# Two-layer decoder trunk on one core: input projection of the unnormalized h, with the norm's factor applied to its banks

## The chip, the cores and the metric

The kernel runs on one core of a Trainium2 chip. The metric is the device time of one execution in microseconds. A core has TensorE (PE in the profile; its weight loads are PEld), VectorE (DVE), ScalarE (ACT), GpSimd (POOL) and SyncE (SP), which here issues every DMA. Each engine has its own queue and works it off in order; an instruction that waits for another engine holds up all that stand behind it. SBUF is the on-chip memory that all of them use; PSUM is where PE's products are summed, in banks of 128 x 512 fp32 numbers.

## The reference

```python
D_MODEL = 1024; SEQ = 1024; DEPTH = 2; NORM_EPS = 1e-6

def rmsnorm(x, g):
    y = x * lax.rsqrt(jnp.mean(x * x, axis=-1, keepdims=True) + NORM_EPS)
    return y * g

for l in range(DEPTH):
    u = rmsnorm(h, attn_norm[l])
    rq, rk, rv, rg, dq, dk, dv = jnp.split(u @ w_in[l], offsets, axis=-1)
    ret  = retention(rq, rk, rv), normed per head, times silu(rg)   # 4 heads
    diff = differential_attention(dq, dk, dv), normed per head      # 4 heads, causal, ALiBi
    h = h + concat(ret, diff) @ w_out[l]
    h = h + swiglu(rmsnorm(h, ffn_norm[l]))
out = rmsnorm(h, final_norm)
```

The line that matters is `u = rmsnorm(h, attn_norm[l])` with the projection behind it. A token's norm factor y = rsqrt(mean(h²) + eps) is one number per token, the gain g one number per channel, so u = h · g · y, and u @ w_in = y · ((h · g) @ w_in), row by row.

## The kernel before, in words

**Layout.** h is kept transposed: eight tiles of 128 channels by 1024 tokens (names a_1 to a_8 and the like in the trace). The tokens are worked in two halves of 512. Products are fp32-accurate ones made of three passes: each operand is split into a rounded high part and the rest (low), and `mm3` issues high x high, high x low and low x high (L268 to L270; L303 to L305 for values, with tokens as rows and 256 columns each). A bank of the projection is thus 8 channel tiles x 3 = 24 products of 512 columns, or 48 of 256 columns. There are three banks called `ps_mm` in rotation for them.

**Weights** come by DMA as raw tiles (`wr`) and are split by `weight`: ACT rounds the high half (L260), POOL subtracts it for the low half (L261).

**The norm** of a half is `norm_half` with two helpers. `squares`: ACT squares each of the eight tiles (L406, into tiles `kb`), DVE adds them up in `acc` (L413). `rsqrt_rows`: PE sums over channels (L378, four matmuls with a column of ones), DVE and ACT make the factor of each token as a column (nx, ny, L383 to L390), PE spreads it by four transposes into a row that is the same on all partitions (L394, in PSUM, `ps_s`). Then `norm_half` makes u: DVE multiplies h · g · y (L426, with y read from PSUM), ACT rounds the high part (L428), DVE subtracts for the low part (L430). The number that its generator yields (lag, gap) is how much other PE work is issued before the row sums and before the transposes.

**What the projection's banks go to.** `stack` takes the q or k bank of a differential head: ACT copies its two halves of 64 rows with a scale (L502) and DVE makes the low parts (L503), all at high priority in the scheduler. `values` copies a bank (ACT, L526) and subtracts (DVE, L527). In the retention `ret_proj` copies the q and k banks (ACT), the values are copied (ACT, L735) and the gates go through ACT's silu (L336).

**Order.** PE's order is written out by hand: generators issue products and yield the number they issued, and `weave(main, n, fill, m)` interleaves two of them in proportion. In `attention` the projection of a head's q and k runs as fill between the parts of the head before. The order on ACT, DVE, POOL and SP is set by a scheduler that follows the program order and priorities.

**The start** of layer 0 is special. `run` loads the weights of the first k and q stacks and half 0 of x in turns; DVE multiplies the gain into these weights (L1195), and `fm_first` (L287) multiplies them with the plain h of half 0, in unsplit fp32, while the norm is being made. When the norm is there, its row is multiplied into the two banks (L672). `keep` gives two of half 0's low parts to POOL. The values of half 0, woven with the norm of half 1, follow, and then head 0, woven with the stacks of half 1.

**From layer to layer**, half 0 of the next layer's norm runs within the last products of the layer before; half 1 is woven with the first stacks of the new layer.

Of the kernel before, what the change touches and what calls it, by code (L numbers as in the profile page):

```python
# [144 lines left out]
class Trunk:  # L145
# [136 lines left out]
    def fm_first(self, h, ws):  # L282

        for w in ws:
            ps = self.bank("mm")
            for k in range(KT):
                self.nc.tensor.matmul(ps, lhsT=w[:, P * k:P * k + P], rhs=h[k][:, 0:HT], start=k == 0,  # L287
                                      stop=k == KT - 1)
                yield 4
            self.first_ps.append(ps)  # L290

# [79 lines left out]
    def rsqrt_rows(self, parts, dim, cols=HT, gap=14):  # L371
# [18 lines left out]
        nc.vector.scalar_tensor_tensor(out=y, in0=x, scalar=1.5, in1=y, op0=ALU.add, op1=ALU.mult)  # L390
        yield gap
# [24 lines left out]
    def norm_half(self, h, hf, gcol, us, lag=11, gap=9, first=False, keep=False):  # L416
        nc = self.nc
        sl = slice(hf * HT, hf * HT + HT)
        parts = self.squares(h, sl, 0, True, first)
        yield lag  # L420
        y = yield from self.rsqrt_rows(parts, D, gap=gap)
        hi = self.t("u", 4, [P, KT, HT], R32)
        lo = self.t("u", 4, [P, KT, HT], R32)
        for k in range(KT):
            f = self.tmp()
            nc.vector.scalar_tensor_tensor(out=f, in0=h[k][:, sl], scalar=self.gains[:, gcol + k:gcol + k + 1],  # L426
                                           in1=y, op0=ALU.mult, op1=ALU.mult)
            nc.scalar.copy(hi[:, k], f)  # L428
            eng = nc.gpsimd if keep and k in (1, 4) else nc.vector
            eng.tensor_tensor(out=lo[:, k], in0=f, in1=hi[:, k].bitcast(F32), op=ALU.subtract)  # L430
        if keep:
            self.first_y = self.big("sp")[:, 0:HT]
            nc.scalar.copy(self.first_y, y)
        us[hf] = (hi, lo)
# [70 lines left out]

    def stacks(self, w, us, halves, st, scale):
        for hf in halves:
            ps = yield from self.fm_half(w, us[hf])
            self.stack(ps, st, slice(hf * HT, hf * HT + HT), scale)
# [8 lines left out]
    def values(self, w2, us, hf, v, pairs=(0, 1)):  # L518
# [4 lines left out]
        for t2 in pairs:  # L523
            ps = yield from self.tm_pair(w2, us[hf], 2 * t2)
            sl = slice(512 * t2, 512 * t2 + 512)
            nc.scalar.copy(h[:, sl], ps)  # L526
            nc.vector.tensor_tensor(out=o[:, sl], in0=ps, in1=h[:, sl].bitcast(F32), op=ALU.subtract)  # L527
# [135 lines left out]
    def attention(self, l, us, w_first, norm1):  # L663
# [5 lines left out]
        if l == 0:  # L669
            for ps, st, scale in zip(self.first_ps, (qk[1], qk[0]), (1.0, 0.125)):  # L670
                f = self.tmp()
                nc.vector.tensor_tensor(out=f, in0=ps, in1=self.first_y, op=ALU.mult)  # L672
                self.stack(f, st, slice(0, HT), scale)
            self.weave(norm1, 40, self.values(wdv, us, 0, v), 48)
# [4 lines left out]
        for h in range(4):  # L679
# [7 lines left out]
            if h == 0:  # L687
                self.weave(self.att_part(l, A, 0, 4), PART0, first[1], 96)
# [23 lines left out]
    def ret_proj(self, us, dst, scale):  # L712
        w = self.weight()
        for hf in range(NH):
            ps = yield from self.fm_half(w, us[hf])
            self.nc.scalar.activation(dst[:, hf * HT:hf * HT + HT], ps, AF.Copy, scale=scale)

    def retention_inputs(self, us, rq, rk, close):
# [8 lines left out]
        for p in range(2):  # L727
            w2, todo = [self.weight(), self.weight()], []
            for hf in range(NH):
                for t2 in range(2):  # L730
                    dst = rv[2 * hf + t2].rearrange("p (t f) -> p t f", t=2)[:, :, 256 * p:256 * p + 256]

                    def go(dst=dst, hf=hf, t2=t2):
                        ps = yield from self.tm_pair(w2, us[hf], 2 * t2)
                        nc.scalar.copy(dst, ps.rearrange("p (t f) -> p t f", t=2))  # L735
# [6 lines left out]
        for h in range(4):  # L742
            w = self.weight()
            for hf in range(NH):
                def go(hf=hf, h=h):
                    ps = yield from self.fm_half(w, us[hf])
                    for c in range(2):
# [430 lines left out]
    def run(self):  # L1178
# [4 lines left out]
        fold = [self.big("sp") for _ in range(2)]  # L1183
# [6 lines left out]
        def load_w(i, c):  # L1190
            cs = slice(512 * c, 512 * c + 512)
            nc.sync.dma_start(raws[i][:, cs], self.a["wts"][i][:, cs])
# [11 lines left out]
        for c in range(2):  # L1204
            load_w(1, c)
# [47 lines left out]
```

## Time and profile before

| | us |
|---|---|
| median of 3 runs | 2317.77 (2315.94 to 2318.31) |
| the profiled execution | 2316.4 |
| its span in the trace | 2314.6 |
| PE busy | 2265.0 (98%) |
| DVE busy | 1389.3 (60%) |
| ACT busy | 1010.4 (44%) |
| POOL busy | 781.0 (34%) |

1.8 us of the profiled execution lie outside the span. In a row of the timeline stand the start, the duration, engine and line, the operation, what it writes and reads, its shape, how often it came in a row, and in brackets the idle time of that engine before it and what ended it. The busy time of a PE instruction (0.39 us for a 512-column product) is longer than the step from one to the next, since they are pipelined; the step is read from the start times. In a table by stretches the columns are the length, then for PE, PEld, DVE, ACT and POOL the busy time and the number of instructions, then the granted clock of PE (1.00 is full), the DMA share and GB/s.

### The profile page before, as it was taken

Reading aid. Unit: us, or ns where it says so; the run is one execution under the profiler, and the core shown is the slowest. Engines: PE = TensorE matmul, PEld = TensorE weight load, DVE = VectorE, ACT = ScalarE, POOL = GpSimd, SP = SyncE. Lnnn points to the kernel's source line nnn. Section 1 sums busy time; section 2 is a strip of 40 time slices with the busy share of each in tenths; the row PEclk is TensorE's granted clock in tenths of the full one; section 3 lists DMA queues with packets and bytes.
Section 4 is the critical chain, followed back from the end, with each engine's and each line's share of the span. In section 5 each row is a group of like instructions: output and inputs, shape, how many; then the busy total and the mean of one; then the engine's idle time right before and its main releaser. Section 6 shows DMA issues by size and latency. Waiting matters only on the chain.

```text
span 2314.6 us, 30688 instructions
## 1 busy us (share of the span) xinstructions
PE 2265.0 (98%) x11328; PEld 1900.0 (82%) x11328; DVE 1389.3 (60%) x2564; ACT 1010.4 (44%) x1905; POOL 781.0 (34%) x620
## 2 busy tenths in 40 slices
PE   8999999998999999999999999999999999999998
PEld 5888898887888888888888888988778888888887
DVE  8777612987534333895567775059874343349856
ACT  5666523444333333543346665234443333344332
POOL 3111212123445455335221112211245445544350
PEclk9999999999999999999999999999999999999999
DMA  4212121111332332652222122212123232346522
GB/s 164 76 47 65 44 94 37 55 56 55 130 116 93 112 105 92 227 195 88 81 84 55 48 72 74 64 37 73 48 91 121 78 128 78 107 162 187 168 64 73
DMA packets 74215, 216.58 MB, mean 94 GB/s; under 512 B 8017, under 2 KB 10065, under 8 KB 74065
## 3 DMA queue, kind: packets, MB, share of 16 engines
q1 hardware_dynamic: 74064, 214.62, 28.7%
q8 instruction: 89, 1.46, 0.3%
q14 instruction: 62, 0.50, 0.1%
HBM read 162.16 MB, written 44.04 MB: 89 GB/s over the span
## 4 chain that ended last, share of the span: by engine, by line
PE 82%; DVE 12%; ACT 3%; issue 2%; DMA 1%; POOL 0%; SPq 0%; DVEq 0%; ACTq 0%; POOLq 0%
PE ps_mm L244 8%; PE ps_mm L246 8%; PE ps_mm L245 8%; PE ps_mm L268 7%; PE ps_mm L269 7%; PE ps_mm L270 7%; PE ps_s L244 5%; PE ps_s L246 5%; PE ps_s L245 5%; PE ps_mm L305 2%; PE ps_mm L303 2%; PE ps_mm L304 2%; PE ps_t L246 2%; PE ps_t L245 2%; PE ps_t L244 2%
## 5 line engine op out<-in xcount | busy, mean ns | idle before, releaser
L221 POOL TENSOR_TENSOR w<-wr,w 128x512 fp32r<-128x512 f32 x286 | 401.9, 1417 | 532.1 <-ACT w L220 492.1
L261 POOL TENSOR_TENSOR w<-wr,w 128x512 fp32r<-128x512 f32 x140 | 184.7, 1326 | 576.9 <-ACT w L260 550.5
L268 PE MATMUL ps_mm<-u,w 128*128 128x512 f32 (+1 forms) x735 | 296.6, 404 | 0.0
L269 PE MATMUL ps_mm<-u,w 128*128 128x512 f32 (+1 forms) x735 | 287.7, 391 | 0.9 <-DVE u L430 0.9
L270 PE MATMUL ps_mm<-u,w 128*128 128x512 f32 (+1 forms) x735 | 287.8, 392 | 0.0
L220 ACT CAST w<-wr 128x512 fp32r<-128x512 f32 x312 | 188.1, 619 | 134.5 <-DVE wr L887 72.0
L245 PE MATMUL ps_mm<-u,w 128*128 128x512 f32 x432 | 168.3, 390 | 0.0
L246 PE MATMUL ps_mm<-u,w 128*128 128x512 f32 x432 | 168.2, 389 | 0.0
L244 PE MATMUL ps_mm<-u,w 128*128 128x512 f32 x432 | 168.2, 389 | 0.0
L270 PEld LDWEIGHTS ps_mm<-u,w 128*128 128x128 f32 x735 | 138.4, 188 | 30.5
L269 PEld LDWEIGHTS ps_mm<-u,w 128*128 128x128 f32 x735 | 138.8, 189 | 24.4 <-DVE u L430 1.2
L268 PEld LDWEIGHTS ps_mm<-u,w 128*128 128x128 f32 x735 | 138.7, 189 | 24.2
L935 ACT COPY t<-ps_mm 128x512 f32<-128x512 f32 x76 | 44.6, 587 | 254.0 <-PE ps_mm L246 254.0
L260 ACT CAST w<-wr 128x512 fp32r<-128x512 f32 x140 | 85.9, 619 | 133.9 <-PE ps_mm L269 42.8
L303 PE MATMUL ps_mm<-w,u 128*128 128x256 f32 x448 | 128.8, 288 | 0.0
L304 PE MATMUL ps_mm<-w,u 128*128 128x256 f32 x448 | 127.7, 285 | 0.0
L305 PE MATMUL ps_mm<-w,u 128*128 128x256 f32 x448 | 127.6, 285 | 0.0
L557 DVE CUSTOM_DVE_ANT_0 sp<-ps_s,wr 128x512 f32<-128x512 f32 (+2 forms) x192 | 103.1, 551 | 35.1 <-PE ps_s L555 34.0
L561 ACT ACTIVATE sp<-sp,m 128x256 f32<-128x256 f32 (+7 forms) x128 | 99.1, 775 | 52.0 <-DVE m L560 51.3
L845 DVE TENSOR_TENSOR a<-a,ps_mm 128x512 f32<-128x512 f32 (+1 forms) x148 | 98.6, 666 | 33.5 <-PE ps_mm L246 20.1
L885 DVE TENSOR_TENSOR t<-wr,wr 128x512 f32<-128x512 f32 x46 | 35.2, 766 | 119.7 <-DMA wr<-wts 119.7
L244 PE MATMUL ps_s<-u,w 128*128 128x512 f32 x264 | 102.9, 390 | 3.4 <-ACT t L935 3.4
(379 smaller groups left out, 5930.9 us busy)
## 6 DMA issues: line engine op xcount, KB each, us to landing
wr<-wts SPq DMA_DIRECT2D x190, 512.0 KB, 3.7
mx<-s_fast SPq DMA_DIRECT2D x56, 512.0 KB, 4.8
s_fast<-mx SPq DMA_DIRECT2D x48, 512.0 KB, 5.0
kb<-ka SPq DMA_DIRECT2D x64, 128.0 KB, 2.3
s_rest<-mx SPq DMA_DIRECT2D x12, 512.0 KB, 2.9
kb<-wts SPq DMA_DIRECT2D x12, 512.0 KB, 5.9
mx<-s_rest SPq DMA_DIRECT2D x12, 512.0 KB, 3.7
a<-xT SPq DMA_DIRECT2D x16, 256.0 KB, 5.4
```

The source lines that it names most:

```text
L220: nc.scalar.copy(h, src)
L221: (eng or nc.gpsimd).tensor_tensor(out=o, in0=src, in1=h.bitcast(F32), op=ALU.subtract)
L244: mm(ps, lhsT=wh[:, c], rhs=bh, start=first and i == 0, stop=False, skip_group_check=True)
L245: mm(ps, lhsT=wh[:, c], rhs=bl, start=False, stop=False, skip_group_check=True)
L246: mm(ps, lhsT=wl[:, c], rhs=bh, start=False, stop=i == 3, skip_group_check=True)
L261: nc.gpsimd.tensor_tensor(out=o, in0=raw[:, cols], in1=h.bitcast(F32), op=ALU.subtract)
L268: mm(out, lhsT=lh, rhs=rh, start=first, stop=False)
L269: mm(out, lhsT=lh, rhs=rl, start=False, stop=False)
L270: mm(out, lhsT=ll, rhs=rh, start=False, stop=last)
L303: mm(o, lhsT=uh, rhs=wh, start=k == 0, stop=False)
L304: mm(o, lhsT=uh, rhs=wl, start=False, stop=False)
L305: mm(o, lhsT=ul, rhs=wh, start=False, stop=k == KT - 1)
```

## The change

- u no longer holds the norm's factor. `norm_half` first makes the high part of h · g on ACT (L416 of the change) and the low part on DVE (L417), for both of which nothing of the norm is needed, and only then squares and sums. The factor is kept twice: as a row (copied from PSUM into an `acc` tile, ACT L423) and as the columns ny.
- Where a bank is read, the factor goes in: the stacks' and gates' banks are multiplied by the row into a `t2` tile first (`normed`, DVE L500, at high priority); `ret_proj` does it in one DVE operation in place of the ACT copy; values and retention values, whose rows are tokens, take a column as the scale (two operations of 256 columns, ACT L525 and DVE L526, in place of one of 512).
- The folded weights and `fm_first` are gone. The first k and q stacks of half 0 are split products like all others, with `weight` called first, and the norm of half 0 is issued between them and the values. POOL has no part in u any more.
- `run` issues the DMAs in another order: all of the first two weights with half 0 of x, then the two values weights, then half 1 of x.

```diff
@@ fm_first (removed)
-        for w in ws:
-            ps = self.bank("mm")
-            for k in range(KT):
-                self.nc.tensor.matmul(ps, lhsT=w[:, P * k:P * k + P], rhs=h[k][:, 0:HT], start=k == 0,
-                                      stop=k == KT - 1)
-                yield 4
-            self.first_ps.append(ps)
@@ rsqrt_rows
+        self.cols = y
         yield gap
@@ norm_half
-    def norm_half(self, h, hf, gcol, us, lag=11, gap=9, first=False, keep=False):
+    def norm_half(self, h, hf, gcol, us, lag=11, gap=9, first=False):
+        hi = self.t("u", 4, [P, KT, HT], R32)
+        lo = self.t("u", 4, [P, KT, HT], R32)
+        us[hf] = [hi, lo, None, None]
+        for k in range(KT):
+            g = self.gains[:, gcol + k:gcol + k + 1]
+            nc.scalar.mul(hi[:, k], h[k][:, sl], g)
+            nc.vector.scalar_tensor_tensor(out=lo[:, k], in0=h[k][:, sl], scalar=g, in1=hi[:, k].bitcast(F32),
+                                           op0=ALU.mult, op1=ALU.subtract)
         parts = self.squares(h, sl, 0, True, first)
         yield lag
         y = yield from self.rsqrt_rows(parts, D, gap=gap)
-        for k in range(KT):
-            f = self.tmp()
-            nc.vector.scalar_tensor_tensor(out=f, in0=h[k][:, sl], scalar=self.gains[:, gcol + k:gcol + k + 1],
-                                           in1=y, op0=ALU.mult, op1=ALU.mult)
-            nc.scalar.copy(hi[:, k], f)
-            eng = nc.gpsimd if keep and k in (1, 4) else nc.vector
-            eng.tensor_tensor(out=lo[:, k], in0=f, in1=hi[:, k].bitcast(F32), op=ALU.subtract)
...
+        row = self.t("acc", 2, [P, 512])
+        nc.scalar.copy(row, y)
+        us[hf][2:] = [row, self.cols]
@@ stacks
+    def normed(self, ps, u):
+        f = self.tmp()
+        with self.tc.high_priority():
+            self.nc.vector.tensor_tensor(out=f, in0=ps, in1=u[2], op=ALU.mult)
+        return f
+
     def stacks(self, w, us, halves, st, scale):
         for hf in halves:
             ps = yield from self.fm_half(w, us[hf])
-            self.stack(ps, st, slice(hf * HT, hf * HT + HT), scale)
+            self.stack(self.normed(ps, us[hf]), st, slice(hf * HT, hf * HT + HT), scale)
@@ values
-            nc.scalar.copy(h[:, sl], ps)
-            nc.vector.tensor_tensor(out=o[:, sl], in0=ps, in1=h[:, sl].bitcast(F32), op=ALU.subtract)
+            for b in range(2):
+                sl, src = slice(512 * t2 + 256 * b, 512 * t2 + 256 * b + 256), ps[:, 256 * b:256 * b + 256]
+                y = us[hf][3][:, 2 * t2 + b:2 * t2 + b + 1]
+                nc.scalar.mul(h[:, sl], src, y)
+                nc.vector.scalar_tensor_tensor(out=o[:, sl], in0=src, scalar=y, in1=h[:, sl].bitcast(F32),
+                                               op0=ALU.mult, op1=ALU.subtract)
@@ attention, layer 0
-            self.weave(norm1, 40, self.values(wdv, us, 0, v), 48)
+            (lag, norm0), norm1 = norm1
+            def main():
+                yield lag
+                yield from norm0
+                for ps, st, scale in zip(got, (qk[1], qk[0]), (1.0, 0.125)):
+                    self.stack(self.normed(ps, us[0]), st, slice(0, HT), scale)
+            self.weave(main(), 96, self.chain(one(wk), one(wq), self.values(wdv, us, 0, v)), 96)
+            next(norm1)
...
-                self.weave(self.att_part(l, A, 0, 4), PART0, first[1], 96)
+                self.weave(self.chain(norm1, self.att_part(l, A, 0, 4)), PART0, first[1], 96)
@@ ret_proj
-            self.nc.scalar.activation(dst[:, hf * HT:hf * HT + HT], ps, AF.Copy, scale=scale)
+            self.nc.vector.scalar_tensor_tensor(out=dst[:, hf * HT:hf * HT + HT], in0=ps, scalar=scale, in1=us[hf][2],
+                                                op0=ALU.mult, op1=ALU.mult)
@@ retention gates
                     ps = yield from self.fm_half(w, us[hf])
+                    ps = self.normed(ps, us[hf])
```

PE at the start. Before, rows from the middle of the second unsplit bank to the first values products (`ps_mm_180` is that bank, `ps_mm_295` a values bank, `acc_155` the squares of half 1):

```order
17 L287 MATMUL ps_mm_180<-a_7_82,sp_87 128x512
18 L287 MATMUL ps_mm_180<-a_8_83,sp_87 128x512
19 L378 MATMUL ps_s_281<-c_ones,acc_155 128x1 x4
20 L303 MATMUL ps_mm_295<-w_248,u_188 128x256
21 L304 MATMUL ps_mm_295<-w_249,u_188 128x256
```

and of the change, from the last products of the q stack to the transposes (`ps_mm_249` is the first values bank, `acc_123` the squares of half 0):

```order
46 L268 MATMUL ps_mm_209<-u_105,w_150 128x512
47 L269 MATMUL ps_mm_209<-u_106,w_150 128x512
48 L270 MATMUL ps_mm_209<-u_105,w_151 128x512
49 L368 MATMUL ps_s_235<-c_ones,acc_123 128x1 x4
50 L293 MATMUL ps_mm_249<-w_156,u_105 128x256
...
73 L295 MATMUL ps_mm_249<-mx_166,u_106 128x256
74 L385 MATMUL ps_s_274<-c_ident,ny_241 128x128 x4
75 L293 MATMUL ps_mm_249<-w_156,u_105 128x256
```

Before, the row sums of half 1 stand ahead of the values; now those of half 0 do, with the transposes 24 products behind, and the sums of half 1 come after the values.

ACT at the end of the values of half 0, in the change (`ps_mm_321` is the second values bank, `kb_412` the last square of half 1):

```order
47 L397 ACTIVATE kb_403<-a_5_80 128x512
48 L397 ACTIVATE kb_406<-a_6_81 128x512
49 L397 ACTIVATE kb_409<-a_7_82 128x512
50 L525 ACTIVATE v_247<-ps_mm_321,ny_241 128x256
51 L199 ACTIVATE c_ex<-c_dots 128x4
52 L397 ACTIVATE kb_412<-a_8_83 128x512
53 L525 ACTIVATE v_247<-ps_mm_321,ny_241 128x256
```

The last square of half 1 stands behind the first copy out of the second values bank.

DVE at the passage from layer 0 to layer 1. Before, around the last add to h (`a_691_3901` is the last tile of h, `acc_9990` the squares of half 1, `u_9818` the low part of half 0):

```order
1243 L426 SCALAR_TENSOR_TENSOR t_1761_9847<-a_691_3901,c_gains,ps_s_9812 128x512
1244 L430 TENSOR_TENSOR u_9818<-t_1760_9843,u_9817 128x512
1245 L413 TENSOR_TENSOR acc_9990<-acc_9990,kb_10007 128x512
1246 L845 TENSOR_TENSOR a_691_3901<-a_691_3901,ps_mm_9925 128x512
1247 L430 TENSOR_TENSOR u_9818<-t_1761_9847,u_9817 128x512
1248 L413 TENSOR_TENSOR acc_9990<-acc_9990,kb_10010 128x512
1249 L383 TENSOR_SCALAR nx_10026<-ps_s_10027 128x4
```

and in the change (`a_696_3964` is that tile, `acc_10057` the squares, `u_10040` the low part of half 1):

```order
1256 L404 TENSOR_TENSOR acc_10057<-acc_10057,kb_10074 128x512
1257 L858 TENSOR_TENSOR a_696_3964<-a_696_3964,ps_mm_9974 128x512
1258 L417 SCALAR_TENSOR_TENSOR u_10040<-a_689_3957,c_gains,u_10039 128x512
1259 L417 SCALAR_TENSOR_TENSOR u_10040<-a_690_3958,c_gains,u_10039 128x512
1260 L404 TENSOR_TENSOR acc_10057<-acc_10057,kb_10077 128x512
1261 L417 SCALAR_TENSOR_TENSOR u_10040<-a_691_3959,c_gains,u_10039 128x512
...
1266 L417 SCALAR_TENSOR_TENSOR u_10040<-a_696_3964,c_gains,u_10039 128x512
1267 L373 TENSOR_SCALAR nx_10093<-ps_s_10094 128x4
```

The operations on half 0 are gone from between the adds; two L417 of half 1 stand ahead of the last add, and six behind it, ahead of the reading of the row sums.

57 lines of the change are left out of this document (17 added, 40 removed).

## The prediction

> **What bounds the kernel now.** I read the page's busy shares first, then what PE waited for over the whole span, then the two stretches in which the long waits lie.
>
> ```profile
> PE 2265.0 (98%) x11328; PEld 1900.0 (82%) x11328; DVE 1389.3 (60%) x2564; ACT 1010.4 (44%) x1905; POOL 781.0 (34%) x620
> ...
> PE ps_s L378 <- DVE acc L413: 8.2, 4, 4.1
> PE ps_mm L287 <- DMA a<-xT: 5.3, 1, 5.3
> PE ps_o L269 <- DVE a L586: 3.3, 8, 0.7
> PE ps_t L580 <- DVE sp L642: 2.5, 2, 1.3
> PE ps_s L554 <- DVE m L557: 1.1, 2, 0.5
> PE ps_mm L269 <- DVE u L430: 0.9, 1, 0.9
> ```
>
> The first line is busy time: PE works 2265.0 of 2314.6 us, so at most 49.6 us of idle time can be won, and beyond that only PE's own work and its clock. In the waits the columns are the sum, the number of waits and the longest. The first is the one that this change is about: PE stands in front of the row sums of squares (L378) because the last add of squares is late, 8.2 us in four places. The two long ones are at the start and at the passage from layer 0 to layer 1:
>
> ```profile
> 5.27 8.24 PE L287 MATMUL ps_mm<-a,sp 128*128 128x512 f32 x12 [5.27 <-DMA a<-xT]
> ...
> 27.82 1.79 PE L378 MATMUL ps_s<-c_ones,acc 128*128 128x1 f32 x8 [2.95 <-DVE acc L413]
> ...
> 31.96 0.41 PE L305 MATMUL ps_mm<-w,u 128*128 128x256 f32 x1
> 32.18 0.41 PE L303 MATMUL ps_mm<-mx,u 128*128 128x256 f32 x1
> ...
> 46.15 0.28 PE L305 MATMUL ps_mm<-mx,u 128*128 128x256 f32 x1
> 46.27 0.40 PE L268 MATMUL ps_mm<-u,w 128*128 128x512 f32 x1
> 46.50 0.40 PE L269 MATMUL ps_mm<-u,w 128*128 128x512 f32 x1
> ```
> ```profile
> 20.00:30.00 10.00, 7.05 (x22) 4.10 (x21) 9.90 (x14) 7.30 (x13) 6.15 (x4) 0.89 0.26 91
> 30.00:40.00 10.00, 9.10 (x48) 8.64 (x47) 9.03 (x18) 4.63 (x9) 3.44 (x3) 0.59 0.54 149
> 40.00:50.00 10.00, 10.00 (x71) 9.35 (x70) 9.91 (x17) 6.31 (x12) 1.02 (x5) 1.00 0.13 34
> ```
>
> The second fence is the table by stretches (length, then busy time of PE, weight loads, DVE, ACT and POOL, then the granted clock). After the wait of 2.95 us the clock was 0.59 for the next 10 us: a 256-column product starts every 0.22 us there (31.96, 32.18) and every 0.12 at 46.15. That is 10 x 0.41 = 4.1 us lost beside the wait itself. DVE is busy for over 9 of 10 us in all three stretches. The first stack of half 1 starts at 46.27, and 0.9 us more is lost in it (the L269 wait above): **47.2 us** is the mark that the changed start has to beat. The step between 512-column products is 0.23 us (46.27, 46.50).
>
> The passage between the layers, PE, then the stretch as a whole, and DVE:
>
> ```profile
> 1159.11 0.40 PE L268 MATMUL ps_mm<-u,w 128*128 128x512 f32 x1
> ...
> 1161.62 0.39 PE L270 MATMUL ps_mm<-u,w 128*128 128x512 f32 x1
> 1166.06 1.83 PE L378 MATMUL ps_s<-c_ones,acc 128*128 128x1 f32 x8 [4.06 <-DVE acc L413]
> ...
> 1169.18 0.63 PE L268 MATMUL ps_mm<-u,w 128*128 128x512 f32 x1
> 1169.61 0.63 PE L269 MATMUL ps_mm<-u,w 128*128 128x512 f32 x1
> ...
> 1171.57 0.60 PE L394 MATMUL ps_s<-c_ident,ny 128*128 128x128 f32 x4
> ```
> ```profile
> 1160.00:1170.00 10.00, 5.94 (x22) 4.84 (x21) 6.57 (x13) 3.40 (x7) 2.75 (x2) 0.73 0.73 247
> ```
> ```profile
> 1158.56 1.77 DVE L413 TENSOR_TENSOR acc<-acc,kb 128x512 f32<-128x512 f32 x1
> ...
> 1163.38 0.68 DVE L845 TENSOR_TENSOR a<-a,ps_mm 128x512 f32<-128x512 f32 x1
> 1163.97 1.34 DVE L430 TENSOR_TENSOR u<-t,u 128x512 fp32r<-128x512 f32 x1
> 1165.23 0.68 DVE L413 TENSOR_TENSOR acc<-acc,kb 128x512 f32<-128x512 f32 x1
> 1167.93 0.16 DVE L383 TENSOR_SCALAR nx<-ps_s 128x4 f32<-128x4 f32 x1 [2.02 <-PE ps_s L378]
> ...
> 1169.00 0.16 DVE L390 SCALAR_TENSOR_TENSOR ny<-nx,ny 128x4 f32<-128x4 f32 x1
> ```
>
> The output products of layer 0 end where the first product of layer 1 starts, 1159.11. Up to the transposes (1171.57) PE needs 12.46 us for 21 products and the row sums. DVE is behind by some 4 us: its adds and the halves' own multiplications and subtractions (L426, L430) stand in one queue, and with two operands in SBUF some took 1.34 to 1.77 us in place of 0.68.
>
> **The change part by part.** The prices, from the groups of the first 60 us (count, sum, mean ns):
>
> ```profile
> L287 PE MATMUL ps_mm<-a,sp 128*128 128x512 f32 x32 | 17.2, 695 | 5.3 <-DMA a<-xT 5.3
> L261 POOL TENSOR_TENSOR w<-wr,w 128x512 fp32r<-128x512 f32 x9 | 13.1, 1462 | 15.4 <-ACT w L260 15.4
> L426 DVE SCALAR_TENSOR_TENSOR t<-a,c_gains,ps_s 128x512 f32<-128x512 f32 x16 | 11.3, 739 | 0.8 <-PE ps_s L394 0.8
> L406 ACT ACTIVATE kb<-a 128x512 f32<-128x512 f32 x14 | 8.7, 628 | 3.3 <-DVE acc L413 1.9 <-DMA a<-xT 1.2
> L260 ACT CAST w<-wr 128x512 fp32r<-128x512 f32 x10 | 6.0, 614 | 6.3 <-PE ps_mm L269 2.4 <-DMA wr<-wts 2.2 <-issue 1.6
> L526 ACT CAST v<-ps_mm 128x512 fp32r<-128x512 f32 x2 | 1.2, 580 | 0.0
> L527 DVE TENSOR_TENSOR v<-ps_mm,v 128x512 fp32r<-128x512 f32 x2 | 1.4, 680 | 0.0
> L672 DVE TENSOR_TENSOR t<-ps_mm,sp 128x512 f32<-128x512 f32 x2 | 1.3, 678 | 0.0
> ```
>
> *Start.* Removed: the unsplit products, 17.2 us of PE, and DVE's folding of the weights. Added: 48 split products, 48 x 0.23 = 11.0 us. So PE has 6.2 us less to do, but it now needs operands that ACT, DVE and POOL make. I lay the new order out in time. PE starts when the first tile is there (5.27) and is split (one ACT operation, 0.63): 5.9. ACT's next twelve operations, casts, squares and splits, take 12 x 0.63 = 7.6, which gives 12.9; the last low part on DVE (priced as L426, 0.74) and late tiles make it 14 to 15, so wk's bank ends at about 15.5. ACT casts the second half of wq as its seventeenth operation, 5.27 + 17 x 0.63 = 16.0; POOL needs 1.46 for it, with a queue ahead, so it is there at 17.5 to 18.2, and the last twelve products of wq end at 21 to 22. The row sums take 1 us, to 22 to 23. The first half of a values bank, 24 x 0.12 = 2.9, ends at 25 to 26. Now the transposes (L385 of the change) wait: between the sums and ny DVE does four L417 of half 1 and four short operations. At 0.74 that is 4 x 0.74 + 0.6 = 3.6 us; at 1.34 (the L430 row at 1163.97, since L417 reads two tiles of SBUF beside POOL's splits) it is 6.0. So ny is ready at 26 to 28.5: **a new wait of 0.5 to 3 us**. Transposes 0.6, the second half 2.9, the second bank 5.7: values end at 35.5 to 38. There the next wait stands: half 1's last square is queued on ACT behind the first copy out of that bank (L525), so after PE's last product come copy (at most 0.58), square 0.63, add 0.68 and the hand-overs, about **2.4 us**. With sums and transposes of half 1 (1.6, which before lay ahead of the mark) the mark is reached at 39.5 to 42 at full clock: 5 to 7.5 us gained. If the wait for L385 is as long as the one of 2.95, the clock can fall as it did there, 4.1 us. Bounds of the gain: 1 and 7.5. I take **4.5**: nearer the upper end, because the longer of the new waits is under 2.95 in the middle of its range.
>
> On that clock the Trainium skill ("TensorE: Matmul & The Clock Gate", What's actually happening) says that the gate closes after about 3.4 us without work, in windows that run freely. By that rule both new waits leave the clock alone and the gain would be 5 to 7.5; the trace agrees only in part, since the 2.95 us above lowered it.
>
> *Passage between the layers.* DVE no longer has L426 and L430 between the adds. After the last product of the output (call it t) come the add to h 0.68, two L417 that are queued ahead (2 x 0.68), the last add 0.68: the sums can start at t + 3.0, where PE's 12 products end at t + 2.8 (12 x 0.23). Nearly all of the 4.06 goes. But six L417 stand ahead of nx on DVE: t + 3.0 + 6 x 0.68 = t + 7.1, then 1.2 us for the chain from nx to ny (1167.93 to 1169.16), t + 8.3, while PE's 9 products end at t + 6.1. So **a new wait of about 2.2** at the transposes, which stand at t + 8.4 to 9.2 in place of t + 12.46. Gain 3.3 to 4.1; with the six L417 at 1.34 it falls by 4 to about 0. I take **3.0**, most of the cover being DVE alone (POOL has 2 operations in 1160 to 1170).
>
> *Banks.* Per layer DVE gets 16 multiplications for the q and k stacks, 8 for the gates and 8 for the retention's q and k (these replace an ACT copy), each 0.68 as L672: 22 us; each values bank becomes two operations of half the size on ACT and two on DVE, which adds about the 0.16 that a tiny operation takes (L390's row). What covers them is PE's own time: 24 products, 5.5 us, to a bank, and three banks. It covers them where DVE has room, and in attention it has little:
>
> ```profile
> 80.00:100.00 20.00, 20.00 (x106) 16.98 (x105) 16.98 (x46) 14.26 (x28) 2.80 (x3) 1.00 0.09 27
> 120.00:140.00 20.00, 18.35 (x98) 14.94 (x97) 18.62 (x60) 14.98 (x33) 2.63 (x2) 1.00 0.10 28
> ```
>
> At 17.0 of 20 us PE has no idle time; at 18.6 it has 1.65. PE's attention waits on DVE (L586, L642, L557 in the first fence) are 6.9 us in 12 waits for both layers. Bounds of the loss: 0, if the new operation always falls between two others, and 12 x 0.68 = 8.2 if each of these waits grows by one of them. I take **2.5**, a third of the present waits, for the fullest stretch only has little room.
>
> On the low parts (L417, L493) the Trainium skill ("SBUF — State Buffer", Who interferes with whom) says that a DVE instruction with two SBUF inputs and a GpSimd instruction that reads SBUF exclude each other. By it those that meet POOL take up to a split longer; the trace agrees: L413, L430 at 1.34 to 1.77, and L426, which reads PSUM, at 0.74 in the same stretch.
>
> *Sum.* −4.5 − 3.0 + 2.5 = −5.0 against the profiled 2316.4 us: 2311.4. The median of the runs is 1.4 above that execution; I predict **2312.5** us.
>
> **The rivals.**
> *All of it comes through.* Neither new wait lowers the clock, DVE's additions hide: −7.5 − 4.1 = −11.6, about 2306. For it: DVE has 40% free over the span. Against: it is full in the first 50 us.
> *The waits only move.* L385 waits 3 us and the clock falls as at 27.82 (gain 1), the six L417 run beside POOL (gain 0.5), attention loses 2.5: +1, about 2318. For it: the rows at 1.34 and 1.77; against: POOL has little to do at the passage.
> *Slower: DVE becomes the bound in attention.* Two banks fall into a stretch like 120 to 140, each with 0.68 and two low parts that now read SBUF (up to 1.3 in place of 0.69): 18.6 + 2 x (0.68 + 1.2) = 22.4 of 20. It decides from about 20 of 20 on. The full 8.2 loss and 4 gained at start and passage: +4 or more, about 2322. For it: PE already waits there for L642. Against: at 17.0 there is no idle, and only one or two stretches of a layer are that full.
>
> **How the numbers follow.** Forecast 0.45, all of it 0.19, waits only move 0.21, slower 0.15. The forecast's own range is 2308 to 2316; the range for 8 in 10 takes in most of the first rival and part of the third: 2304.5 to 2321. About 0.2% (4.6 us) can be told from no change: faster is below 2313.1, just over half of the forecast's case and the first rival, 0.45; slower above 2322.4 holds half of the last rival's case and a tail, 0.14; the same 0.41.
>
> **What would show it.** L368 of half 0 with no wait over 1 us; a wait at L385 of 0.5 to 3 us near 25 us and one of about 2.4 at L368 near 37; the first stack of half 1 free at 40 to 43; a clock of 1.00 in 30 to 40. At the passage, under 1 us at L368 and about 2.2 at L385. In attention, PE's waits on L642, L586 and L557 summing to about 9. It is wrong if attention's waits grow by more than 6, if the start is not free before 45, or if PE waits for a bank that L500 has not read.

## The result, and the profile after

The changed kernel takes **2334.76 us** in the median (2332.69 to 2335.21, 4 runs) against 2318.04 before (2315.94 to 2318.38, 4 runs): 1.0072 times as long (95% interval 1.0059 to 1.0084). It is 16.7 us slower; 2312.5 was forecast, with a range up to 2321. The profiled execution has a span of 2333.3 us, 18.7 more than before. In two of the runs told below one execution was disturbed and is left out of the times: 7986 us with a row of ones, which is the traced one, so that none of its rows is read, and 12880 us with the row in PSUM.

Of the changed kernel, the page's busy times and the shares of the chain that ended last (the work followed back from the last instruction, at each step to what released it), then what PE waited for (sum, times, longest). The last line of the first fence is that chain before:

```profile
PE 2265.2 (97%) x11344; PEld 1900.8 (81%) x11344; DVE 1422.6 (61%) x2608; ACT 1016.0 (44%) x1924; POOL 776.6 (33%) x618
...
PE 75%; DVE 15%; ACT 4%; issue 3%; DMA 2%; POOL 1%; SPq 0%; DVEq 0%; ACTq 0%; POOLq 0%
...
PE 82%; DVE 12%; ACT 3%; issue 2%; DMA 1%; POOL 0%; SPq 0%; DVEq 0%; ACTq 0%; POOLq 0%
```
```profile
PE ps_t L580 <- DVE sp L642: 12.3, 8, 2.1
PE ps_s L554 <- DVE m L557: 9.5, 11, 1.4
PE ps_mm L268 <- ACT u L416: 6.2, 1, 6.2
PE ps_s L385 <- DVE ny L380: 6.1, 4, 1.9
...
PE ps_s L368 <- DVE acc L404: 4.0, 5, 2.0
PE ps_o L269 <- DVE a L586: 3.6, 8, 0.7
```

PE's busy time is the same to 0.2 us, so all of the loss is waiting or what goes with it. The wait for the squares (before L378, now L368) fell from 8.2 to 4.0, as meant. The two waits of attention that stood at 2.5 and 1.1 us are now 12.3 and 9.5: the transposes of the softmax (L580) wait for L642, the scores (L554) for the reading of an earlier bank (L557). In the chain DVE's share rose from 12% to 15%.

Where it came is seen from the time at which PE starts the first scores of a head. The last column is the run without the stacks' row multiplication, told below.

| us from the start | before | changed | difference | no row in the stacks |
|---|---|---|---|---|
| layer 0, head 1 | 110.79 | 110.04 | −0.75 | 105.54 |
| layer 0, last scores | 283.98 | 292.26 | +8.28 | 279.41 |
| layer 1, head 0 | 1193.78 | 1200.05 | +6.27 | 1186.55 |
| layer 1, last scores | 1426.06 | 1443.02 | +16.96 | 1419.77 |
| end of the span | 2314.59 | 2333.31 | +18.72 | 2308.85 |

So attention loses 9.0 us in layer 0 (head 1 on) and 10.7 in layer 1. Start and passage do gain. PE's rows of the start and the stretches there:

```profile
6.16 0.80 PE L268 MATMUL ps_mm<-u,w 128*128 128x512 f32 x1 [6.16 <-ACT u L416]
...
24.18 0.38 PE L294 MATMUL ps_mm<-w,u 128*128 128x256 f32 x1 [0.91 <-POOL w L261]
28.63 0.65 PE L385 MATMUL ps_s<-c_ident,ny 128*128 128x128 f32 x4 [1.90 <-DVE ny L380]
41.39 1.02 PE L368 MATMUL ps_s<-c_ones,acc 128*128 128x1 f32 x8 [1.99 <-DVE acc L404]
42.27 0.48 PE L268 MATMUL ps_mm<-u,w 128*128 128x512 f32 x1
```
```profile
30.00:40.00 10.00, 9.40 (x67) 9.19 (x65) 9.29 (x17) 6.88 (x14) 1.02 (x5) 0.84 0.03 10
40.00:50.00 10.00, 8.61 (x37) 7.10 (x38) 2.29 (x9) 2.60 (x7) 1.48 (x2) 0.83 0.23 53
```

The two new waits are where they were expected, 1.90 us at the transposes of half 0 and 1.99 at the sums of half 1; the first stack of half 1 starts at 42.27, where 47.2 was the mark. A wait that was not expected, 0.91 us for a weight's low part on POOL (L261), stands at 24.18. At the passage, PE and then DVE:

```profile
1172.71 1.02 PE L368 MATMUL ps_s<-c_ones,acc 128*128 128x1 f32 x8 [1.24 <-DVE acc L404]
...
1177.81 0.62 PE L385 MATMUL ps_s<-c_ident,ny 128*128 128x128 f32 x4 [1.88 <-DVE ny L380]
```
```profile
1169.37 2.58 DVE L417 SCALAR_TENSOR_TENSOR u<-a,c_gains,u 128x512 fp32r<-128x512 f32 x2
1171.88 0.68 DVE L404 TENSOR_TENSOR acc<-acc,kb 128x512 f32<-128x512 f32 x1
1172.48 4.05 DVE L417 SCALAR_TENSOR_TENSOR u<-a,c_gains,u 128x512 fp32r<-128x512 f32 x6
1176.46 0.14 DVE L373 TENSOR_SCALAR nx<-ps_s 128x4 f32<-128x4 f32 x1
```

One wait of 4.06 us has become two of 1.24 and 1.88, and the clock no longer falls there.

### The profile page after: what moved, and what is told of

It reads as the page before. It is cut to its first block, busy times and chain, and to the rows that moved or that the text cites. A ratio compares the mean times of both kernels' runs of the same rounds, so it can differ in the third digit from the quotient of the medians.

```text
span 2333.3 us, 30792 instructions
## 1 busy us (share of the span) xinstructions
PE 2265.2 (97%) x11344; PEld 1900.8 (81%) x11344; DVE 1422.6 (61%) x2608; ACT 1016.0 (44%) x1924; POOL 776.6 (33%) x618
## 4 chain that ended last, share of the span: by engine, by line
PE 75%; DVE 15%; ACT 4%; issue 3%; DMA 2%; POOL 1%; SPq 0%; DVEq 0%; ACTq 0%; POOLq 0%
PE ps_mm L244 8%; PE ps_mm L245 7%; PE ps_mm L246 7%; PE ps_mm L268 5%; PE ps_mm L269 5%; PE ps_mm L270 5%; PE ps_s L246 5%; PE ps_s L244 5%; PE ps_s L245 5%; PE ps_mm L295 2%; PE ps_mm L294 2%; PE ps_mm L293 2%; PE ps_t L246 2%; PE ps_t L245 2%; PE ps_t L244 2%
## 5 line engine op out<-in xcount | busy, mean ns | idle before, releaser
L261 POOL TENSOR_TENSOR w<-wr,w 128x512 fp32r<-128x512 f32 x140 | 186.2, 1336 | 630.8 <-ACT w L260 607.3
L268 PE MATMUL ps_mm<-u,w 128*128 128x512 f32 x751 | 304.3, 405 | 6.2 <-ACT u L416 6.2
L270 PE MATMUL ps_mm<-u,w 128*128 128x512 f32 x751 | 295.1, 393 | 0.5 <-POOL w L261 0.5
L269 PE MATMUL ps_mm<-u,w 128*128 128x512 f32 x751 | 295.3, 393 | 0.0
L245 PE MATMUL ps_mm<-u,w 128*128 128x512 f32 x432 | 168.5, 390 | 0.0
L244 PE MATMUL ps_mm<-u,w 128*128 128x512 f32 x432 | 168.4, 390 | 0.0
L246 PE MATMUL ps_mm<-u,w 128*128 128x512 f32 x432 | 168.4, 390 | 0.0
L270 PEld LDWEIGHTS ps_mm<-u,w 128*128 128x128 f32 x751 | 142.1, 189 | 31.7 <-POOL w L261 0.9
L268 PEld LDWEIGHTS ps_mm<-u,w 128*128 128x128 f32 x751 | 142.5, 190 | 31.1 <-ACT u L416 6.2
L269 PEld LDWEIGHTS ps_mm<-u,w 128*128 128x128 f32 x751 | 142.5, 190 | 25.1 <-DVE u L417 1.2
L561 ACT ACTIVATE sp<-sp,m 128x256 f32<-128x256 f32 (+7 forms) x128 | 98.9, 773 | 78.1 <-DVE m L560 77.5
L557 DVE CUSTOM_DVE_ANT_0 sp<-ps_s,wr 128x512 f32<-128x512 f32 (+2 forms) x192 | 103.2, 551 | 28.1 <-PE ps_s L555 26.7
L500 DVE TENSOR_TENSOR t<-ps_mm,acc 128x512 f32<-128x512 f32 x48 | 32.9, 687 | 142.9 <-PE ps_mm L270 142.7
L858 DVE TENSOR_TENSOR a<-a,ps_mm 128x512 f32<-128x512 f32 (+1 forms) x148 | 98.6, 666 | 29.3 <-PE ps_mm L246 17.2
```

The costliest lines, as they stand in the source:

```text
L244: mm(ps, lhsT=wh[:, c], rhs=bh, start=first and i == 0, stop=False, skip_group_check=True)
L245: mm(ps, lhsT=wh[:, c], rhs=bl, start=False, stop=False, skip_group_check=True)
L246: mm(ps, lhsT=wl[:, c], rhs=bh, start=False, stop=i == 3, skip_group_check=True)
L261: nc.gpsimd.tensor_tensor(out=o, in0=raw[:, cols], in1=h.bitcast(F32), op=ALU.subtract)
L268: mm(out, lhsT=lh, rhs=rh, start=first, stop=False)
L269: mm(out, lhsT=lh, rhs=rl, start=False, stop=False)
```

## How attention loses 20 us

Three stretches of attention, with the length, the busy time of PE, PEld, DVE, ACT and POOL, and the clock. The first fence is the third stretch in the kernel before (the prediction shows the other two), the second is the changed kernel:

```profile
160.00:180.00 20.00, 20.00 (x167) 19.88 (x166) 10.72 (x32) 8.44 (x23) 0.74 (x4) 1.00 0.05 18
```
```profile
80.00:100.00 20.00, 19.85 (x106) 16.49 (x105) 17.19 (x40) 14.70 (x27) 3.52 (x4) 1.00 0.20 52
120.00:140.00 20.00, 14.91 (x78) 11.91 (x77) 17.83 (x55) 12.70 (x27) 2.88 (x2) 1.00 0.10 28
160.00:180.00 20.00, 17.89 (x149) 17.63 (x148) 10.63 (x20) 10.60 (x20) 2.26 (x5) 1.00 0.18 55
```

PE idles most where DVE is nearly full, 5.09 us in 120 to 140, but not only there. In 160 to 180 DVE is busy for 10.6 of 20 us and PE idles for 2.11. What happens there is told by the chain of waits (start, time, what; pieces left out are marked) and the row of PE at its end, both of the changed kernel:

```profile
158.05 0.66 DVE mx L613
...
158.78 0.60 DVE sp L557
...
159.39 0.60 DVE t L500
159.99 0.60 DVE sp L557
...
160.63 1.16 DVE a L586 x2
...
161.80 0.69 DVE a L493
...
162.50 0.69 DVE a L493
...
163.20 0.16 DVE z L562
...
163.45 0.96 ACT sp L561
...
164.69 1.05 ACT sp L634
...
165.76 1.29 DVE sp L642
...
167.19 0.85 PE ps_t L580 x6
```
```profile
167.19 1.06 PE L580 MATMUL ps_t<-c_ident,sp 128*128 128x128 f32 x8 [2.11 <-DVE sp L642]
```

The softmax of a block is a chain: read the scores (L557), take the maximum, exponentiate on ACT (L561), scale (L634), combine (L642), transpose on PE (L580). The row multiplication L500 stands on DVE between the two halves of one block's scores, and the stack's low parts (L493) between the scores and the rest. Each is short, and each stands in this chain with its full time. DVE rests later, when it waits for ACT; that rest is of no use to the chain.

## The experiments

Theory A: the row multiplication of the stacks is what costs. Its rival B: what else the change does in attention.

The clock has a part in some of the times. The table counts it as the prediction does, 10 us times what the granted clock lacks of full in each stretch of 10 us, over the two attentions (50 to 300 and 1180 to 1480 us) of each run's traced execution. What the run lost by it is at most this, since PE also waits in these stretches.

| run | clock lacks, us | | run | clock lacks, us |
|---|---|---|---|---|
| before | 0.0 | | plain priority | 12.0 |
| changed | 0.0 | | unread multiplication | 1.7 |
| no row in the stacks | 0.0 | | half of it | 1.7 |
| row in PSUM | 3.4 | | double of it | 11.9 |
| low parts on POOL | 7.3 | | changed, with DMAs | 1.7 |

**Without the row in the stacks.** The scores are then left unnormalized.

```diff
-            self.stack(self.normed(ps, us[hf]), st, slice(hf * HT, hf * HT + HT), scale)
+            self.stack(ps, st, slice(hf * HT, hf * HT + HT), scale)
```

> The changed kernel without the multiplication by the norm's row in the q and k stacks (16 of 32 row multiplications per layer; their scores are left unnormalized, and the low parts read PSUM again). Theory A, the row multiplication of the stacks is what PE waits for in attention: the waits of PE at L580 and L554 fall from 21.8 us to under 8, and the time from 2334.8 to 2314 to 2319. Theory B, the loss comes from what else the change does in attention (head 0's weave without fill at its end, two operations for one on the values, another order on DVE and ACT): at least 2328. Between 2320 and 2327 both have a share.

Measured 2311.78 (2309.88 to 2314.66, 10 runs), ratio to before 0.9973 (0.9964 to 0.9983). So 23.0 us go with the 32 multiplications in both layers, and what is left of the change is a gain of 6.3, though the gates' and the retention's multiplications are still in it. The low parts read PSUM again in this run, at 689 and 690 ns in place of 873 and 722 in layer 0's attention, so the 23.0 hold that as well. The waits at L580 and L554:

```profile
PE ps_t L580 <- DVE sp L642: 3.3, 4, 1.3
...
PE ps_s L554 <- DVE m L557: 1.1, 2, 0.5
```

They are back at 4.4 us from 21.8. The time is a little better than A's span, and B is out as the main cause.

**The kernel before, with a row of ones in the stacks.**

```diff
             ps = yield from self.fm_half(w, us[hf])
+            f = self.tmp()
+            with self.tc.high_priority():
+                v = lambda t: t.rearrange("p (n c) -> p n c", c=P)
+                one = self.ones.bitcast(F32).rearrange("p (n c) -> p n c", n=1).broadcast_to([P, 4, P])
+                self.nc.vector.tensor_tensor(out=v(f), in0=v(ps), in1=one, op=ALU.mult)
-            self.stack(ps, st, slice(hf * HT, hf * HT + HT), scale)
+            self.stack(f, st, slice(hf * HT, hf * HT + HT), scale)
```

> The kernel before with one part of the change alone: each q and k bank that goes through the stacks (14 of 16 in layer 0, 16 in layer 1) is first multiplied by a row, here of ones, into a temporary tile at high priority, so the result is unchanged. Theory A: PE's waits at L580 and L554 grow as in the changed kernel and the time rises by 13 to 21 us, to 2331 to 2339. Theory B: it rises by less than 5 us, to at most 2323.

Measured 2341.93 (2340.48 to 2342.29, 3 runs), ratio 1.0102 (1.0085 to 1.0118): 23.9 us more, above even A's span. That one part, put into the kernel before, costs more than the whole change does.

**The row multiplied in place in PSUM** (the gates' banks too, since they go through the same `normed`).

```diff
-            self.nc.vector.tensor_tensor(out=f, in0=ps, in1=u[2], op=ALU.mult)
-        return f
+            self.nc.vector.tensor_tensor(out=ps, in0=ps, in1=u[2], op=ALU.mult)
+        return ps
```

> The changed kernel with the row multiplied in place, the product written back to the PSUM bank, so that the stacks' low parts (L493) read PSUM and one SBUF tile in place of two SBUF tiles. If a good part of the loss is that L493 shares SBUF with POOL (873 and 722 ns in the attention of layer 0 in place of 689), L493 returns to 0.69 us and 3 to 8 us are won: 2327 to 2332. If the time of the multiplication itself decides: within 2 us of 2334.8.

Measured 2329.30 (2328.21 to 2333.61, 3 runs), ratio 1.0056 (1.0035 to 1.0076): 5.5 us won by the medians, inside the span expected if the low parts' SBUF reading is a good part of the loss, though the interval overlaps that of the changed kernel. L493 is back at 689 ns, and PE's two waits fell:

```profile
PE ps_t L579 <- DVE m L559: 4.6, 2, 2.3
PE ps_s L553 <- DVE m L556: 4.4, 4, 2.1
...
PE ps_t L579 <- DVE sp L641: 2.7, 4, 1.0
```

With a last 0.9 for L585, these are 12.6 us in place of 21.8, while the clock lacked 3.4 us. So some 5 us of the loss may go with where the product stands; three runs that spread over 5.4 us do not size it.

**Low parts on POOL.**

```diff
-                nc.scalar.activation(st[j][a, sl], ps[a], AF.Copy, scale=scale)
-                nc.vector.scalar_tensor_tensor(out=st[j][b, sl], in0=ps[a], scalar=scale,
-                                               in1=st[j][a, sl].bitcast(F32), op0=ALU.mult, op1=ALU.subtract)
+                nc.scalar.copy(st[j][a, sl], ps[a])
+                nc.gpsimd.tensor_tensor(out=st[j][b, sl], in0=ps[a], in1=st[j][a, sl].bitcast(F32), op=ALU.subtract)
...
-            self.nc.vector.tensor_tensor(out=f, in0=ps, in1=u[2], op=ALU.mult)
+            self.nc.vector.scalar_tensor_tensor(out=f, in0=ps, scalar=scale, in1=u[2], op0=ALU.mult, op1=ALU.mult)
```

> The changed kernel with the scale taken into the row multiplication and the stacks' low parts made on POOL, so that a bank costs DVE one operation of 0.7 us, against 3 in the changed kernel and 2 before. Theory A (DVE's time in attention decides): PE's waits at L580 and L554 fall below those of before (3.6 us), and the time falls by 14 to 24 us, to 2311 to 2321. Its rival, that POOL's operations hold up DVE's with two SBUF inputs as much as they relieve it: 2328 or more. Theory B: within 3 us of 2334.8.

Measured 2333.2, ratio 1.0070 (1.0055 to 1.0085): no change, outside A's span and as its rival had it. From 90 to 290 us of the traced execution (2338.4, the longest of four) DVE was busy for 145.0 us in place of 154.5, but POOL for 67.4 in place of 35.0, and the waits moved: those at the transposes and scores fell from 21.8 to 11.4, those at L269 grew from 3.6 to 10.0. Two groups on DVE and POOL in that stretch, and the first of PE's waits:

```profile
L357 DVE TENSOR_TENSOR t<-t,t 128x512 f32<-128x512 f32 x7 | 6.8, 965 | 0.1
...
L493 POOL TENSOR_TENSOR ka<-t,ka 64x512 fp32r<-64x512 f32 x11 | 15.9, 1447 | 9.0 <-ACT ka L492 8.4
```
```profile
PE ps_o L269 <- DVE a L585: 10.0, 11, 2.2
```

L357 takes 965 ns in the mean, in the changed kernel 688: two of its seven, with two SBUF inputs, began while POOL was subtracting and took 1.67 and 1.68 us, the others 0.67 to 0.69. That is the rule of the Trainium skill ("SBUF — State Buffer", Who interferes with whom), and the trace agrees. It need not account for all of the missing gain: the clock has up to 7.3 us in it, in the changed kernel none. These two and the low parts' coming later from POOL are not parted, so the run decides nothing about A.

Is it then DVE's time (A1), the place that high priority gives it (A2), or the hand-over from DVE to ACT's copies (A3)?

**Plain priority** for the row (the gates' too), the copies and the low parts.

```diff
-        with self.tc.high_priority():
-            self.nc.vector.tensor_tensor(out=f, in0=ps, in1=u[2], op=ALU.mult)
+        self.nc.vector.tensor_tensor(out=f, in0=ps, in1=u[2], op=ALU.mult)
...
-            with self.tc.high_priority():
+            with nullcontext():
```

> The changed kernel with the row multiplications and the stacks' copies and low parts at plain priority, so that the scheduler need not put them ahead of the softmax's operations on DVE and ACT. Theory A1, each operation that DVE has more per bank costs its own time wherever it stands: within 3 us of 2334.8. Theory A2, it costs because high priority puts it between two links of the softmax chain: at most 2329.

Measured 2345.92, ratio 1.0123 (1.0108 to 1.0138): 11 us worse than the changed kernel, which neither theory had. A2 falls: the priority was a help. A1 as it stood (its own time wherever it stands, within 3 us) is too simple as well. The stretch from 90 to 290 us of this run:

```profile
90.00:290.00 200.00, 186.10 (x1043) 160.02 (x1042) 152.53 (x420) 120.36 (x248) 34.92 (x45) 0.97 0.19 51
```

DVE is busy for 152.5 us there, in the changed kernel for 154.5, so it is no busier; but the clock is 0.97 in place of 1.00, and over both attentions it lacked 12.0 us in place of none. So the worse place may cost by way of the clock. The other executions of this run had a mean clock of 0.993 to 0.994 in place of 0.990 and were no faster, so how much of the 11 us that is stays open.

**A multiplication that nobody reads**, in the kernel before: as in the run with ones, but the stacks read the bank.

> The kernel before with the same multiplication of each stack bank by ones at high priority, but into a tile that nobody reads: the stacks read the bank as before, so neither ACT's copies nor the low parts wait for it. If DVE's time there decides (A1, A2): 2334 to 2342, near the 2342.1 of the run in which the stacks read the product. If what decides is the longer hand-over, ACT's copies waiting in their queue for DVE (A3): at most 2328.

Measured 2335.04, ratio 1.0078 (1.0063 to 1.0093): 16.9 us for DVE time that no copy or low part waits for by its data, and the same two waits of PE (lines are shifted by 5: L585 are the transposes, L559 the scores); the group of the multiplication is the last row:

```profile
PE ps_s L559 <- DVE m L562: 9.1, 8, 1.4
...
PE ps_t L585 <- DVE sp L647: 6.3, 4, 2.4
```
```profile
L513 DVE TENSOR_TENSOR t<-ps_mm,c_ones 128x512 f32<-128x512 f32 x30 | 20.4, 684 | 1.5 <-PE ps_mm L270 1.2
```

A3 falls as the main cause: 16.9 of the 23.9 us come without it. The other 7.0 belong to the stacks' reading the product: a later hand-over, or SBUF inputs, which the run with the row in PSUM puts near 5; the two are not parted. In the 16.9 is also a new wait of 2.1 us, of values' products (L303) for L503.

**Half and double of it.** Two runs with the unread multiplication at 128x256 and with two of them per bank.

> The kernel before with the unread multiplication at half the width (128x256, 0.35 to 0.4 us in place of 0.68), 30 of them. If the price is in proportion from the first tenth of a microsecond: 2318 plus 8 to 10, 2325 to 2329. If there is some room that is used up first: at most 2322.

> The kernel before with two unread multiplications per bank in place of one (60, 41 us of DVE). In proportion to the run with one (2335.0, so 17 for 30): 2318 plus 34, 2349 to 2355. Growing faster, as a queue that fills up does: over 2355. Some of them hidden: under 2347.

Measured: half 2331.81, ratio 1.0059 (1.0044 to 1.0075), above both spans that were expected; double 2354.0, ratio 1.0155 (1.0141 to 1.0169), in the span in proportion. The half-width operation takes 418 ns:

```profile
L513 DVE TENSOR_TENSOR t<-ps_mm,c_ones 128x256 f32<-128x256 f32 x30 | 12.5, 418 | 0.8 <-PE ps_mm L270 0.5
```

So 12.5 us of DVE cost 14.0, 20.4 cost 16.9 and 41.0 cost 36.2. There is no room to be used up first: 0.8 to 1.1 of the time of the added operations came out at the end. That the price is in proportion to the time is not shown. Half the time cost only 2.9 us less, each value is uncertain by some 3.5, and a fixed part for every operation that stands there would fit as well. DVE's whole busy time rose by more than the operations' own, by 18.9, 28.2 and 43.1 us. Of the 36.2, moreover, up to 11.9 came through the clock, of the other two at most 1.7.

**One copy, one low part and four DMAs per bank**, in the changed kernel.

```diff
+        hi, lo = self.tmp(R32), self.tmp(R32)
+        with self.tc.high_priority():
+            nc.scalar.activation(hi, ps, AF.Copy, scale=scale)
+            nc.vector.scalar_tensor_tensor(out=lo, in0=ps, scalar=scale, in1=hi.bitcast(F32), op0=ALU.mult,
+                                           op1=ALU.subtract)
         for j in range(2):
             a, b = slice(64 * j, 64 * j + 64), slice(64 - 64 * j, 128 - 64 * j)
-            with self.tc.high_priority():
-                ...
+            nc.sync.dma_start(st[j][a, sl].bitcast(F32), hi[a].bitcast(F32))
+            nc.sync.dma_start(st[j][b, sl].bitcast(F32), lo[a].bitcast(F32))
```

> The changed kernel with the stacks' two copies and two low parts of 64 rows made as one copy and one low part of 128 rows in temporary tiles, which four DMAs per bank then put in their places. With the row multiplication DVE then has two operations per bank, as many as before, and ACT one in place of two. A1: PE's waits at L580 and L554 return to under 8 us and the time to 2310 to 2317. A3: at least 2328. Its own risk, that the places are filled too late or SP's queue is held up: new waits of PE on DMA, and 2318 to 2330.

Measured 2314.29 (2312.70 to 2317.44, 10 runs), ratio 0.9987 (0.9978 to 0.9997): 20.5 us below the changed kernel and just below the kernel before. With as many DVE operations per bank as before, the loss is gone; ACT has one copy per bank less as well, which is not parted from it. PE's waits in attention (now L583 and L557) are 8.5 and 1.0, a little over what was expected, and no wait on the DMAs is among them:

```profile
PE ps_t L583 <- DVE sp L645: 8.5, 7, 2.3
...
PE ps_s L557 <- DVE m L560: 1.0, 2, 0.5
```

**The same stacks in the kernel before.**

> The kernel before with the stacks' copies and low parts as in the run with four DMAs per bank: one copy on ACT and one operation on DVE in place of two and two. It tells what of the gain there belongs to the change and what to the DMAs alone. PE's attention waits on DVE before are 6.9 us. If a DVE operation per bank has its price also downward: 2311 to 2315. If before has enough room on DVE: 2317 to 2319, and then the changed kernel with DMAs is the better of the two by what it gains at start and passage.

Measured 2312.82, ratio 0.9981 (0.9972 to 0.9990): 5.0 us won. DVE is busy for 15.2 us less (1374.1 in place of 1389.3), and that gains 5.0; the 28.2 us more with the unread multiplication cost 16.9. PE's attention waits on DVE were only 6.9 us before, so less could be won there than lost; that this is the reason is argued, not shown. The changed kernel with DMAs (2314.29) is not the better of the two; their intervals overlap.

**Three low parts of layer 1's half 0 on POOL**, in the kernel before.

```diff
-            eng = nc.gpsimd if keep and k in (1, 4) else nc.vector
+            eng = nc.gpsimd if (keep and k in (1, 4)) or k in pool else nc.vector
```

> The kernel before with three of the eight low parts of layer 1's half 0 (L430, tiles 1, 4 and 6) given to POOL, as two of layer 0's are: does DVE's backlog at the passage make the wait of 4.06 us? If so, 3 operations of 0.7 to 1.5 us less ahead of the last add: the wait falls by 2 or more and the time by 2 to 5 us, to 2313 to 2316. If POOL's subtractions hold up DVE's as long as they relieve it: 2317 to 2320.

Measured 2316.74, ratio 0.9996 (0.9986 to 1.0006): no difference, and between the two spans, though near the second. The longest wait at L378 went from 4.06 only to 3.2; the backlog at the passage is not made by these three alone, or POOL gives part of it back.

**Norm's small operations at high priority**, on top of the changed kernel with DMAs: the lines of `rsqrt_rows` from the row sums to ny go under `self.tc.high_priority()`.

> The changed kernel with four DMAs per bank, and the norm's small operations (sums to ny, on DVE and ACT) at high priority, so that at the passage one L417 in place of six stands ahead of the reading of the row sums, and the rest is interleaved. If the six L417 make the wait at the transposes (1.9 us at the passage, 1.9 at the start), these waits fall below 0.9 each and the time from 2314.3 to 2310 to 2313. If the low parts that are put off hold up the next products instead: 2314 to 2317.

Measured 2311.29 (2310.86 to 2312.87, 6 runs), ratio 0.9971 (0.9959 to 0.9982), the lowest median of all the runs. At the passage the transposes' wait is small:

```profile
1159.32 1.03 PE L368 MATMUL ps_s<-c_ones,acc 128*128 128x1 f32 x8 [1.30 <-DVE acc L405]
1162.89 0.63 PE L386 MATMUL ps_s<-c_ident,ny 128*128 128x128 f32 x4 [0.34 <-DVE ny L381]
```

From the sums to the transposes it is now 3.57 us (1159.32 to 1162.89), in the changed kernel 5.10 (1172.71 to 1177.81) and in the run with DMAs alone 5.11 (of which only 0.44 was waiting; the clock was 0.83 there), which bears out that the six L417 ahead of nx made that wait. At the start it stayed at 1.90; there the priority changed nothing. Against the kernel before with DMAs (2312.82) the intervals overlap: that the changed projection is worth anything once the stacks are cheap is not shown, and the kernel before with DMAs was not run with this priority.

## Why the prediction was wrong

- **Start: the size was right, its effect smaller.** 4.5 was taken. The first stack of half 1 starts at 42.27 against the mark of 47.2, with 0.6 of transposes still to come: 4.3 gained. The two waits, 1.90 and 1.99, lay within the stated 0.5 to 3 and near 2.4. By head 1 it is 0.75: the clock was at half for two spells of 3.4 us (0.84 and 0.83 in the two rows above, 1.6 to 1.7 us each, where the sign named was 1.00 in 30 to 40). The second spell lies behind the mark, and of the rest head 0, whose stacks have the row too, is the likely place. Without the stacks' row it is 5.25 at head 1. The working fits closely: the products of wq ended at 21.4, the transposes began at 28.6. Three small slips in it change nothing: twelve ACT operations from 5.9 end at 13.5, not 12.9; twelve products from 17.5 to 18.2 end at 20.3 to 21.0; and 2311.4 with 1.4 added is 2312.8.
- **Passage: the gain was right.** 3.0 taken. Where the output products of layer 0's end begin (L268 on `ps_t`), the changed kernel is 9.3 us behind (1100.53 against 1091.23); at head 0 of layer 1 it is 6.27 behind, so 3.0 are won. The sums waited 1.24 us, where t + 3.0 against t + 2.8 gives 0.2 and the sign said under 1; the transposes 1.88 in place of 2.2. The two L417 ahead of the last add took 2.58 in place of 1.36, beside POOL.
- **Banks: the step that failed.** "Bounds of the loss: 0 … and 12 x 0.68 = 8.2", with 2.5 taken. Measured: 23.0 by taking the stacks' multiplication out, 19.7 between the marks of the table above. PE's waits on L642, L557 and L586 were to sum to about 9, and growth by more than 6 was the sign of being wrong; they grew from 6.9 to 25.4. The upper bound let only the 12 waits that the trace before showed grow, by one operation each. But PE has no wait where the chain of a block happens to arrive just in time, and there were many such places: 19 waits at L580 and L554 in place of 4. "What covers them is PE's own time: 24 products" was the wrong cover: it hides when a bank is read, not what the reading does to the softmax operations behind it on DVE. Without this term the rest of the change came to −6.3, where −7.5 was forecast for start and passage.
- **The slower rival had the right place and engine, but another mechanism and about a third of the price.** It named attention and DVE, with a loss of 8.2 there and a chance of 0.15, and had DVE full; what the runs show is a chain that grows longer with DVE partly idle. Its threshold, 20 of 20 us in a stretch, is refuted by 160 to 180, where DVE was half idle.
- **The first look** at the stretch of 17.0 of 20, "at 17.0 of 20 us PE has no idle time", took the average for a margin. In the changed kernel it still has only 0.15 us of idle there at 17.2; the waits came at other loads, above and far below.

## What to carry to other kernels

Where a chain runs through several engines for every block, take the price of one more operation on one of them to be its whole time, until the chain is shown to have room. Here it was 0.8 to 1.1 of that, and the busy share of the engine did not show it, high or low. Before moving a factor from operands (once) to results (once per bank), count how often the result is read and on whose chain. A cheap way to learn the price is to put the operation into the kernel as it is, on data that nobody reads.

## What was not expected of the hardware

- Waits of 1.90 and 1.99 us at the start were each followed by about 3.4 us at half clock, while at the passage 1.24 and 1.88, five microseconds apart, left it at full (the stretch of the passage, with 1.00 behind the busy times):

```profile
1170.00:1180.00 10.00, 6.89 (x36) 5.31 (x35) 7.78 (x14) 1.90 (x6) 2.63 (x7) 1.00 0.43 150
```

  The Trainium skill ("TensorE: Matmul & The Clock Gate", What's actually happening) speaks of an idle window of about 3.4 us; here waits of 1.90 and 1.99 us, amid work, were followed by the fall, and the measurement decides.
- In the traced execution of the run with DMAs and priority the granted clock was 0.95 in nearly every stretch (0.945 in the mean); the other five executions show 0.995 or 0.996. The step of the products stayed at 0.23 us, and its time, 2311.09, is among theirs (2310.86 to 2312.87). So this lower figure went with no loss of time; what it means is open:

```profile
699.69 0.39 PE L245 MATMUL ps_s<-u,w 128*128 128x512 f32 x1
699.91 0.39 PE L246 MATMUL ps_s<-u,w 128*128 128x512 f32 x1
```
